# The second token group's sixteen gate tiles as three fp32r products of high and low parts

## The chip, the cores and the metric

The kernel runs on one core of a Trainium2 chip. The metric is the device time of one execution in microseconds (us). Five engines work side by side, each on its own queue of instructions in order: TensorE (PE, whose weight loads appear as PEld), VectorE (DVE), ScalarE (ACT), GpSimd (POOL) and SyncE (SP), which here only issues DMA transfers.

## The reference, cut to what matters

One layer of a hybrid decoder, for 512 prompt tokens and 64 sample tokens, model width 1024, float32 throughout:

```python
proj = x @ w_in
q, k, v, u, ga, gb = jnp.split(proj, SPLIT_IDX, axis=-1)      # ga, gb: 1024 columns each
a = attn_prompt(q, k, v, attn_sinks)                          # or attn_sample
s, hr, hi = ssm_branch(u, ...)
mix = jax.nn.sigmoid(ga) * (a @ w_attn_proj) + jax.nn.sigmoid(gb) * (s @ w_ssm_proj)
x = layer_norm(DN_ALPHA * x + mix @ w_out, ln1_g, ln1_b)
x = layer_norm(DN_ALPHA * x + peer(x, ...), ln2_g, ln2_b)
x = x + jax.nn.sigmoid(x @ ple_w_gate) * (p @ ple_w_proj)
```

The change concerns `sigmoid(ga)` and `sigmoid(gb)`. `peer` takes for each token the best 16 keys of two sets of 128 for each of 8 heads, the best 16 of their pair sums, and 128 experts that these name: a row of `u_tab` and one of `v_tab` for each.

## The kernel before, in words

The 576 tokens are two groups. Group A has 192 tokens (64 sample tokens and the first prompt block), group B has 384 (three prompt blocks of 128). Both go through the same steps, A first; B's steps are laid beside A's where the program allows it. Activations lie transposed, as 128 rows by 8 chunks by tokens.

**Gates.** `gate` (lines 526 to 531) makes `sigmoid(ga)` in eight tiles of 128 gate columns and `gate1` (lines 533 to 538) `sigmoid(gb)` in eight more, which only group B does this way. Each tile loads 128 x 1024 float32 weights (512 KB, `wload`, line 431, from a pool of six buffers), multiplies them with `g.xT` in eight chunks of 128 (`mm`, line 402, plain float32) into one PSUM tile of lane B, and ACT writes the sigmoid. The profile lists each plain float32 matmul as two records: the 128 matmuls of the sixteen tiles are 256 records. `g.xT` is B's input, 128 x 8 x 384 float32.

**Products of parts.** Elsewhere B's products are made of parts: ACT copies a float32 tile to the shorter format fp32r (the high part, line 213), DVE subtracts it from the tile (the low part, line 216), and three products are summed in PSUM: high with high, high with low, low with high (`mm3`, line 409; `parts` makes the two halves of a weight tile in lane H, whose pool `ws["H"]` has four buffers, two weight tiles with both halves). So the attention and SSM projections (`mix0`, `mix1`), the output projection (`out`, line 637), the PEER queries (`peerq`, 15 of its 16 tiles) and the experts (`up`, `dense`, lines 1127 and 1254) are made. `mix0` first makes parts of the attention output (`at`, line 543 and following, tag "xl" of the pool `xp`).

**Rows.** For the first two token blocks (A's) the experts' rows are gathered one at a time: POOL issues an indirect DMA of 128 rows of 4 KB (512 KB, line 1064) into one of four buffers and DVE reduces it (line 1074, later 1083). These reductions are pinned to their order in the program. `pull(n)` writes n of them at a place in the program: two for each tile of `gate1` (PG = 2), one for each of the eight tiles of `mix0`, 1.5 for each of the eight of `mix1` and of the eight steps of `out`. That is 16 + 8 + 12 + 12 = 48 up to the end of `out`. The other 336 follow later, most of them beside the dense experts.

**Order.** The main program around the change is, in the order in which it is written: A's PEER queries (`peerq`, with `topk_sides`, lines 959 to 963, after each quarter: the best 16 of each set of keys, on DVE); A's `topk` for the second block (`run(A.topk(tk, (1,)))`), whose last result is the row indices `idx` (line 1018) on which the first gather waits; B's `gate` with steps of A's `topk` for the first block beside it; B's `gate1` with the rows; `load_y`, `glu`, `mix0`, `mix1`, `out`; then `ln1`, `project` (line 937), `peerq` and `topk` for B, the experts (`first`, `dense`) and the last layer norm. The framework fixes the order of each engine's instructions when the program is built, and may put later work ahead of earlier work that isn't ready. At run time each engine takes its queue strictly in that order.

**Memory.** B's tiles of 128 x 4 x 384 have the tag "mB" with four buffers: `qT`, `AT`, `yT`, `sT`. The pool `xp` (xB) is opened once A's pools are closed, in memory that A's tiles held; it has two buffers of 128 x 8 x 384, "xh" (first `g1`, the result of `gate1`) and "xl" (first `at`). The pool `wH1`, lane H's buffers for `mix0`, `mix1` and `out`, is opened after `glu`.

Of the kernel before, what the change touches and what calls it, by code (L numbers as in the profile page):

```python
# [7 lines left out]
FP = mybir.dt.float32  # L8
# [5 lines left out]
FR = mybir.dt.float32r  # L14
AF = mybir.ActivationFunctionType
# [184 lines left out]
def build(tc, I, O, dbg=None):  # L200
    nc = tc.nc
    V, S, G, T, SY = nc.vector, nc.scalar, nc.gpsimd, nc.tensor, nc.sync
    mult, add, sub = ALU.mult, ALU.add, ALU.subtract
# [5 lines left out]
    def act(out, in_, fn, **k):  # L209
        S.activation(out, in_, fn, **k)  # L210

    def copy(out, in_):
        S.activation(out, in_, AF.Copy)  # L213

    def tt(out, a, b, op, e=None):
        return (e or V).tensor_tensor(out, a, b, op=op)  # L216

    with (
# [172 lines left out]
        def phase1(pools):  # L391
            (c1, wk, gp, ws) = pools
            if 1:
# [24 lines left out]
                class Lane:  # L418

                    def __init__(l, name, cols):  # L420
                        l.name, l.cols = name, cols
# [27 lines left out]
                class Group:  # L449
                    def __init__(g, d, pool, ga):  # L450
                        g.__dict__.update(d)
                        g.first = g.name == "A"
                        g.pool = pool
                        g.ln = LA if g.first else LB
                        g.xT = g.big("xT")
                        SY.dma_start(g.xT, I["xT" + g.name])
                        g.cs = ga.tile([128, 2, g.N], FP, name="cs" + g.name)
                        g.qT = g.med("qT")
                        g.kT = gp.tile([128, g.N], FP, name="kT" + g.name)
                        g.Vn = {}  # L460

# [61 lines left out]
                                    S.dma_start(O["kp"], t)  # L523


                    def gate(g):

                        g.mx = g.big("mix")
                        for n in range(8):
                            act(g.mx[:, n], g.mm(g.ln.wload(I["w_in"][10 + n]), g.xT, 8), AF.Sigmoid)  # L530
                            yield

                    def gate1(g, xp):

                        g.g1 = xp.tile([128, 8, g.N], FP, name="g1", tag="xh")
                        for n in range(8):
                            act(g.g1[:, n], g.mm(g.ln.wload(I["w_in"][18 + n]), g.xT, 8), AF.Sigmoid)
                            yield

                    def half(g, w, n, x):  # L540
# [816 lines left out]
        left, right = ExitStack(), ExitStack()  # L1357

        def open_(st, name, bufs=1, side="left", **k):
            return st.enter_context(tc.tile_pool(name=name, bufs=bufs, side=side, **k))  # L1360
# [4 lines left out]
        ws = {"B": wb}  # L1365
        setup = ssm_setup()
        next(setup)
        Group, LA, LB, consts, project, (ssm_U, ssm_X, ssm_states, ssm_Y) = phase1((c1, wk, gp, ws))
        A = Group(GA, ga, ga)
        w = [LB.wload(I["w_in"][6])]  # L1370
        B = Group(GB, gp, ga)
# [30 lines left out]
        def beside(work, n):  # L1402
            for _ in work:
                due[1] += n
                while due[1] >= 1:
                    due[1] -= 1
                    next(sb, 0)
# [55 lines left out]
        xp = open_(xB, "xB", 1, "right")  # L1463
        rows.extend(gathered_rows(bi, gt, wk2) for bi in (1, 0))
        run(A.topk(tk, (1,)))
        sb = A.topk(tk, (0,))
        due[1] = 0
        beside(B.gate(), T0)
        for _ in B.gate1(xp):
            pull(PG)  # L1470
        B.load_y()
        beside(B.glu(), T1)
        wH1 = ExitStack()
        ws["H"] = open_(wH1, "wH1", 4, "right")
        for _ in B.mix0(xp):
            due[1] += T2
            while due[1] >= 1:
# [60 lines left out]
```

## Time and profile before

| | |
|---|---|
| median of 3 runs | 1915.37 us (1914.25 to 1915.6) |
| profiled execution | 1914.61 us, its span 1912.8 us |
| mean granted clock of TensorE | 0.972 of full speed |
| PE busy | 94% of the span |
| DVE busy | 77% |
| ACT busy | 40% |
| POOL busy | 31% |
| B's gates up to the end of `out` | from about 383 to 553 us |
| experts that only PE bounds | from about 945 to 1645 us |

The profile is of one execution. Busy time is the time in which an engine had an instruction under way. An idle time is put down to what ended it last. The granted clock is 1.00 at 2.4 GHz and 0.50 at 1.2 GHz. The shares over the whole span say little here, because the stages have different limits; the windows by stage say more.

### The profile page before, as it was taken

The page shows a single profiled execution, that of the slowest core. Times are in us where ns is not written, and L with a number is a line of the kernel's source. Part 1 is how long each engine was busy: PE and PEld are TensorE (multiplying, and loading weights), DVE is VectorE, ACT ScalarE, POOL GpSimd, SP SyncE. Part 2 cuts the span into 40 slices and gives each one's busy share as a digit, 9 for nine tenths or more (in the row PEclk, how much of TensorE's full clock was granted, in tenths as well). Part 3 has the DMA queues.
Part 4 walks back from the last instruction along what each step waited for, and adds up shares of the span by engine and source line. Part 5 has one row for each costly group of instructions (what it writes and reads, how often), then busy time and mean ns, then how long its engine had stood idle before and what let it go on. Part 6 is the DMA issues. An engine that isn't in the chain of part 4 may idle for free.

```text
span 1912.8 us, 26365 instructions
## 1 busy us (share of the span) xinstructions
PE 1805.5 (94%) x9506; PEld 1551.1 (81%) x9506; DVE 1480.8 (77%) x2965; ACT 768.6 (40%) x1144; POOL 585.7 (31%) x437
## 2 busy tenths in 40 slices
PE   6789999999898989999999999999999999999998
PEld 5668897855768847888899999999999999877886
DVE  8261235697997898998678888888888888798885
ACT  2112443142232237797833333333333333344332
POOL 4110000007341210000035554444446566343220
PEclk9888999999899989999999999999999999999999
DMA  6743446338886366676899999999999999999952
GB/s 205 239 149 91 169 149 216 105 127 306 311 308 246 124 205 212 235 253 229 300 348 358 353 348 342 339 341 344 339 348 335 347 338 332 327 396 360 378 187 75
DMA packets 207795, 512.29 MB, mean 268 GB/s; under 512 B 33328, under 2 KB 99904, under 8 KB 205600
## 3 DMA queue, kind: packets, MB, share of 16 engines
q1 hardware_dynamic: 142608, 303.28, 44.6%
q0 software_dynamic: 56160, 204.78, 29.7%
q10 hardware_dynamic: 8896, 2.56, 0.5%
q8 instruction: 74, 1.21, 0.2%
q14 instruction: 57, 0.47, 0.1%
HBM read 461.34 MB, written 50.71 MB: 268 GB/s over the span
## 4 chain that ended last, share of the span: by engine, by line
PE 66%; DVE 15%; DMA 8%; ACT 5%; issue 4%; POOL 1%; SPq 0%; ACTq 0%; DVEq 0%; POOLq 0%
PE psA L1254 12%; PE psB L1254 12%; PE psB L1127 11%; PE psA L1127 11%; PE psA L402 6%; DMA g<-u_tab,idx 3%; PE psB L402 2%; ACT Gs L210 2%; DVE eq L216 2%; PE psA L637 2%; DMA fr<-w_gate 2%; PE psA L409 1%; DVE s L216 1%; DMA ur<-u_t 1%; PE psA L937 1%
## 5 line engine op out<-in xcount | busy, mean ns | idle before, releaser
L1064 POOL DMA_INDIRECT g<-u_tab,idx x192 | 285.4, 1486 | 748.3 <-DVE scr L1074 454.8
L1064 POOL DMA_INDIRECT g<-v_tab,idx x192 | 256.6, 1336 | 343.5 <-DVE acc L1083 303.1
L1074 DVE SCALAR_TENSOR_TENSOR scr<-g,x 128x1024 bf16<-128x1024 f32 x192 | 234.1, 1219 | 28.5 <-DMA g<-u_tab,idx 26.8
L1083 DVE SCALAR_TENSOR_TENSOR acc<-g,hh,acc 128x1024 f32<-128x1024 f32 x190 | 244.7, 1288 | 6.5 <-DMA g<-v_tab,idx 4.8
L213 ACT ACTIVATE vh<-vr 128x1024 fp32r<-128x1024 f32 x128 | 135.8, 1061 | 161.3 <-PE psB L1254 141.5
L216 DVE TENSOR_TENSOR ul<-ur,uh 128x1024 fp32r<-128x1024 f32 x120 | 146.6, 1223 | 67.2 <-ACT uh L213 64.6
L213 ACT ACTIVATE uh<-ur 128x1024 fp32r<-128x1024 f32 x120 | 127.0, 1062 | 155.7 <-PE psA L1127 72.8
L216 DVE TENSOR_TENSOR vl<-vr,vh 128x1024 fp32r<-128x1024 f32 x128 | 156.0, 1219 | 10.7 <-ACT vh L213 10.7
L1254 PE MATMUL psA<-vh,wh 128*128 128x512 f32 x384 | 151.1, 393 | 5.8 <-ACT wh L213 5.8
L1254 PE MATMUL psA<-vl,wh 128*128 128x512 f32 x384 | 150.1, 391 | 0.0
L1254 PE MATMUL psB<-vl,wh 128*128 128x512 f32 x384 | 150.1, 391 | 0.0
L1254 PE MATMUL psB<-vh,wh 128*128 128x512 f32 x384 | 150.0, 391 | 0.0
L1254 PE MATMUL psB<-vh,wl 128*128 128x512 f32 x384 | 150.0, 391 | 0.0
L1254 PE MATMUL psA<-vh,wl 128*128 128x512 f32 x384 | 149.4, 389 | 0.0
L213 ACT ACTIVATE wh<-wt 128x384 fp32r<-128x384 f32 x128 | 67.0, 524 | 181.1 <-DVE wt L216 144.9
L402 PE MATMUL psB<-xTB,w 128*128 128x384 f32 x400 | 132.9, 487 | 0.0
L216 DVE TENSOR_TENSOR wl<-wt,wh 128x384 fp32r<-128x384 f32 x128 | 71.2, 556 | 57.8 <-ACT wh L213 48.7
L402 PEld LDWEIGHTS psB<-xTB,w 128*128 128x128 f32 x400 | 75.0, 190 | 48.9 <-issue 0.6
L1127 PE MATMUL psB<-xh,uh 128*128 128x384 f32 x480 | 96.9, 344 | 5.0 <-ACT Gs L210 4.5
L1127 PE MATMUL psA<-xh,uh 128*128 128x384 f32 x480 | 95.2, 339 | 3.9 <-ACT uh L213 3.9
L210 ACT ACTIVATE Gs<-psB 128x512 f32<-128x512 f32 x96 | 94.9, 1150 | 7.9 <-PE psB L1174 7.9
L1127 PE MATMUL psA<-xl,uh 128*128 128x384 f32 x480 | 95.3, 337 | 0.0
(370 smaller groups left out, 3775.8 us busy)
## 6 DMA issues: line engine op xcount, KB each, us to landing
ur<-u_t SPq DMA_DIRECT2D x128, 512.0 KB
vr<-v_tab SPq DMA_DIRECT2D x128, 512.0 KB
Gg<-Gs SPq DMA_DIRECT2D x12, 2048.0 KB
G<-Gg SPq DMA_DIRECT2D x32, 768.0 KB
w<-w_in SPq DMA_DIRECT2D x42, 512.0 KB
w<-w_q SPq DMA_DIRECT2D x32, 512.0 KB
w<-w_out SPq DMA_DIRECT2D x16, 512.0 KB
Hd<-gl SPq DMA_DIRECT2D x42, 192.0 KB
```

Of the source, the lines that this page charges most:

```text
L210: S.activation(out, in_, fn, **k)
L213: S.activation(out, in_, AF.Copy)
L216: return (e or V).tensor_tensor(out, a, b, op=op)
L402: T.matmul(out, w[:, k, :], x[:, k, :], start=(k == 0), stop=(k == kc - 1))
L409: T.matmul(out, a[:, k], b[:, k], start=f and k == 0, stop=l and k == kc - 1)
L637: T.matmul(p[bi][:n], a[:, k + i, c0:c0 + n], b[:, i], start=f and i == 0, stop=e and i == 1)
L937: T.matmul(p, t[bi // 4][:, bi % 4, k], w[hf][:, k], start=(k == 0), stop=(k == 1))
L1064: G.indirect_dma_start(out=t, out_offset=None, in_=I[tab], in_offset=bass.IndirectOffsetOnAxis(ap=IDX[bi][:, i:i + 1], axis=0))
L1074: pin(V.scalar_tensor_tensor(scr, t, 1.0, X1[bi], op0=mult, op1=mult, accum_out=hh[:, i:i + 1]))
L1083: pin(V.scalar_tensor_tensor(acc, t, hh[:, i:i + 1], acc, op0=mult, op1=add))
L1127: T.matmul(p, w[:, c * 128:c * 128 + 128], z[:, c], start=f and c == 0, stop=l and c == 7)
L1254: T.matmul(y[b][hf], x[:, bs], z[:, hf * 512:hf * 512 + 512], start=f, stop=l)
```

## The change

B's gate tiles become sums of three fp32r products. `xparts` splits B's input once: the high part goes into two tiles with the tag "mB" (taken when the group is made, ahead of `AT`, `yT` and `sT`), the low part into the buffer "xl" of `xp`. Each gate tile's weights are split by `parts` into lane H's buffers, so the pool `wH1` is opened ahead of the gates. Group A's gates stay as they were.

```diff
@@ Group.__init__
                         g.qT = g.med("qT")
+                        if not g.first:
+                            g.xTh = [g.pool.tile([128, 4, g.N], FR, tag="m" + g.name, name="xTh", bufs=4) for _ in range(2)]
                         g.kT = gp.tile([128, g.N], FP, name="kT" + g.name)
@@ methods of Group
+                    def xparts(g, xp):
+
+                        lo = xp.tile([128, 8, g.N], FR, name="xTl", tag="xl")
+                        for k in range(0, 8, 2):
+                            hi, sl = g.xTh[k // 4][:, k % 4:k % 4 + 2], slice(k, k + 2)
+                            copy(hi, g.xT[:, sl])
+                            tt(lo[:, sl], g.xT[:, sl], hi.bitcast(FP), sub)
+                        g.xp = [g.xTh[k // 4][:, k % 4] for k in range(8)], [lo[:, k] for k in range(8)]
+
+                    def gates(g, w):
+
+                        raw = g.ln.wload(w)
+                        if g.first:
+                            return g.mm(raw, g.xT, 8)
+                        p = g.ln.ps(g.N)
+                        (wh, wl), (xh, xl) = parts(raw), g.xp
+                        for a, b, f, l in ((wh, xh, True, False), (wh, xl, False, False), (wl, xh, False, True)):
+                            for k in range(8):
+                                T.matmul(p, a[:, k], b[k], start=f and k == 0, stop=l and k == 7)
+                        return p
+
                     def gate(g):
 
                         g.mx = g.big("mix")
                         for n in range(8):
-                            act(g.mx[:, n], g.mm(g.ln.wload(I["w_in"][10 + n]), g.xT, 8), AF.Sigmoid)
+                            act(g.mx[:, n], g.gates(I["w_in"][10 + n]), AF.Sigmoid)
                             yield
 
                     def gate1(g, xp):
 
                         g.g1 = xp.tile([128, 8, g.N], FP, name="g1", tag="xh")
                         for n in range(8):
-                            act(g.g1[:, n], g.mm(g.ln.wload(I["w_in"][18 + n]), g.xT, 8), AF.Sigmoid)
+                            act(g.g1[:, n], g.gates(I["w_in"][18 + n]), AF.Sigmoid)
                             yield
@@ main program
         due[1] = 0
+        wH1 = ExitStack()
+        ws["H"] = open_(wH1, "wH1", 4, "right")
+        B.xparts(xp)
         beside(B.gate(), T0)
         for _ in B.gate1(xp):
             pull(PG)
         B.load_y()
         beside(B.glu(), T1)
-        wH1 = ExitStack()
-        ws["H"] = open_(wH1, "wH1", 4, "right")
         for _ in B.mix0(xp):
```

## Rows read from the trace of the kernel before

**Rows 1.** The page's busy time by engine: busy us (share of span) xinstructions.

```profile
PE 1805.5 (94%) x9506; PEld 1551.1 (81%) x9506; DVE 1480.8 (77%) x2965; ACT 768.6 (40%) x1144; POOL 585.7 (31%) x437
```

**Rows 2.** Windows by stage: busy us (instructions) of each engine, granted clock, DMA share.

```profile
core 0: us, PE busy (x) PEld busy (x) DVE busy (x) ACT busy (x) POOL busy (x), PEclk, DMA share, GB/s
...
316.00:383.00 67.00, 67.00 (x374) 55.47 (x373) 37.56 (x215) 14.82 (x34) 0.00 (x0) 1.00 0.35 115
383.00:421.00 38.00, 38.00 (x120) 22.50 (x121) 37.04 (x200) 14.45 (x17) 0.00 (x0) 1.00 0.28 92
421.00:455.00 34.00, 34.00 (x107) 20.06 (x106) 29.48 (x87) 13.74 (x17) 21.38 (x15) 1.00 0.84 296
455.00:466.00 11.00, 11.00 (x38) 6.79 (x37) 7.55 (x13) 2.79 (x5) 7.88 (x5) 1.00 0.82 282
466.00:510.00 44.00, 34.52 (x181) 33.80 (x179) 40.16 (x72) 10.98 (x13) 21.33 (x19) 0.91 0.87 316
510.00:553.00 43.00, 38.61 (x153) 30.94 (x153) 39.19 (x61) 9.00 (x10) 22.23 (x19) 0.89 0.92 319
```

**Rows 3.** Waits of DVE, 383 to 553 us: us in total, times, longest.

```profile
DVE scr L1074 <- DMA g<-u_tab,idx: 11.5, 7, 3.5
DVE VE L959 <- ACT sc L213: 4.5, 1, 4.5
DVE st L216 <- ACT st L213: 3.3, 1, 3.3
```

**Rows 4.** Timeline of PE: start, us, instruction xrecords; gate matmuls of B.

```profile
316.38 6.62 PE L402 MATMUL psB<-xTB,w 128*128 128x384 f32 x20
...
323.56 0.91 PE L402 MATMUL psB<-xTB,w 128*128 128x384 f32 x2
...
383.18 71.76 PE L402 MATMUL psB<-xTB,w 128*128 128x384 f32 x222
```

**Rows 5.** Chain that ended last: start, us; 24 fp32r matmuls of an expert tile.

```profile
972.64 4.17 PE psA L1127 x24
```

**Rows 6.** Groups of DVE, 383 to 553 us: busy, mean ns | idle before.

```profile
L1074 DVE SCALAR_TENSOR_TENSOR scr<-g,x 128x1024 bf16<-128x1024 f32 x48 | 58.4, 1217 | 11.9 <-DMA g<-u_tab,idx 11.5
L216 DVE TENSOR_TENSOR wl<-w,wh 128x1024 fp32r<-128x1024 f32 x16 | 19.4, 1218 | 0.0
...
L216 DVE TENSOR_TENSOR at<-ATB,at 128x1536 fp32r<-128x1536 f32 x1 | 1.8, 1759 | 0.3 <-ACT mixB L210 0.3
```

**Rows 7.** Timeline of ACT: a copy to high parts of each size.

```profile
383.94 1.47 ACT L213 ACTIVATE at<-ATB 128x1536 fp32r<-128x1536 f32 x1
...
445.61 1.06 ACT L213 ACTIVATE wh<-w 128x1024 fp32r<-128x1024 f32 x1 [0.32 <-DMA w<-w_ap]
```

**Rows 8.** Timeline of DVE: key maxima of B's first query quarter, then weight splits.

```profile
600.21 0.49 DVE L959 MAX8 VE<-sc 128x8 f32<-128x128 f32 x2 [0.42 <-ACT sc L213]
...
612.61 0.28 DVE L959 MAX8 VE<-sc 128x8 f32<-128x128 f32 x1
613.78 1.22 DVE L216 TENSOR_TENSOR wl<-w,wh 128x1024 fp32r<-128x1024 f32 x1
```

**Rows 9.** Timeline of PE: the matmuls that waited for that split.

```profile
615.05 2.93 PE L409 MATMUL psA<-xh,wl 128*128 128x384 f32 x8 [2.66 <-DVE wl L216]
```

**Rows 10.** Timeline of DVE, 404 to 421 us: A's second topk, its last result.

```profile
404.64 1.00 DVE L216 TENSOR_TENSOR eq<-eq,CI 128x1664 uint16<-128x1664 uint16 x1
...
419.95 0.21 DVE L1018 CAST idx<-ef 128x128 int32<-128x128 f32 x1
```

**Rows 11.** Timeline of PE: the first matmuls after the wait in `mix0`.

```profile
479.14 2.93 PE L409 MATMUL psB<-at,wh 128*128 128x384 f32 x8 [5.55 <-ACT wh L213]
```

**Rows 12.** Timeline of POOL: GLU's copies behind gathers; a gather issue beside a weight split.

```profile
474.78 1.84 POOL L616 COPY sTB<-ev 128x384 f32<-128x384 f32 x4
483.87 1.70 POOL L1064 DMA_INDIRECT g<-u_tab,idx  x1 [7.25 <-DVE scr L1074]
486.61 0.94 POOL L1064 DMA_INDIRECT g<-u_tab,idx  x1 [1.04 <-DVE scr L1074]
```

**Rows 13.** Timeline of SP's queue: weight loads of the gates and of GLU.

```profile
371.80 52.54 SPq L431 DMA_DIRECT2D w<-w_in  x9
429.17 5.49 SPq L431 DMA_DIRECT2D w<-w_glu  x2
```

## The prediction, made before the changed kernel ran

> **What bounds the kernel now.** The page's first part comes first: PE is busy for 94% of the span and DVE for 77% [rows 1]. Taken alone, that says that any PE time saved is time saved. The windows by stage correct it [rows 2]. While the gates run, from 383 to 455 us, PE has no gap, but from 383 to 421 us DVE is busy for 37.04 of 38 us as well: it is at group A's top-k. From 466 to 553 us both have gaps, 13.9 us on PE and 7.65 us on DVE. Over the 170 us from 383 to 553 us, PE is busy for 38.00 + 34.00 + 11.00 + 34.52 + 38.61 = 156.1 us and DVE for 37.04 + 29.48 + 7.55 + 40.16 + 39.19 = 153.4 us. The two are level, and what the change takes from the one it gives to the other. DVE's 16.6 us of idle time in this stretch are mostly 11.5 us of waiting for gathered rows and one wait of 3.3 us for the GLU result [rows 3]. The wait of 4.5 us in the same list lies nearly all before 383 us. What follows 553 us on the path (B's layer norm, queries, top-k, experts) needs B's output projection, so a shift of that point goes through to the end.
>
> **What it removes.** 128 plain matmuls. A block of 222 records, or 111 matmuls, takes 71.76 us [rows 4], so one takes 0.646 us and all take 82.7 us. In their place come 384 fp32r matmuls of the same 128 x 384 shape. Twenty-four of these take 4.17 us in the expert stage at full clock [rows 5], or 0.174 us each: 66.7 us in all. PE's work falls by 16.0 us. The Trainium skill (FP8 and Floating Point Precision, section TensorE Precision Notes) counts plain float32 as four passes through the array, so that three single passes would save a quarter, 20.7 us as an estimate. The rows decide for 16.0: each pass of its own costs some 12 ns more than a quarter of a plain matmul.
>
> **What it moves on PE.** Of the gate matmuls 34 records, 17 matmuls, run before 383 us: one block of 20 records at 316 us, while A's layer norm is under way and PE has nothing else, and seven pairs slipped between A's queries [rows 4]. After the change a gate tile can't start there: its low parts lie in memory that A's pools hold until A's queries are done, near 383 us. So 17 x 0.646 = 11.0 us of PE work lose their place. The seven pairs, 4.5 us, no longer delay A's queries, which end near 378.5 us. PE alone would have 66.7 us of gates from there, and would end them at about 446 us (1 us to start) in place of 455 us.
>
> **What it adds on DVE.** Sixteen weight splits of 1.218 us [rows 6]. Neighbouring instructions overlap by some 0.07 us, so 1.15 us each and 18.4 us in all. Four splits of the input, 128 x 768: by the 1.759 us for 128 x 1536 [rows 6], 0.88 us each and 3.5 us in all. Together 21.9 us. The split of the attention output (1.76 us, now before 421 us) moves behind the last gate tile, because it shares the buffer "xl" with the input's low part; it stays within the stretch. Its 1.47 us copy on ACT and these 1.76 us are then due right after the gates, where GLU's matmuls, the 11 us from 455 to 466 us in [rows 2], cover them.
>
> **What it adds on ACT.** Sixteen copies of 1.06 us and four of 1.47 / 2 = 0.74 us [rows 7], 19.9 us. ACT is busy for 14.45 + 13.74 of 72 us there [rows 2]. I cost this at nothing: the cover is ACT's 44 us of idle time. If a copy stood in the queue ahead of a top-k step, it would add about 1 us to that step.
>
> **Queues.** SP's nine loads of gate weights from 371.8 us wait for raw buffers, and GLU's loads stand behind them [rows 13]. A raw buffer is now free after its split, not after its matmuls, so these loads wait for DVE, but no bytes are added. I cost it at nothing; its other bound is the time by which the splits are late, which is counted with DVE already. POOL gets no new instruction.
>
> **The sum.** DVE does its queue in order, and in the query stage of B the trace shows whose turn it is. The key maxima hold DVE from 600.21 to 613.78 us without one weight split among them, and PE waits 2.66 us for that split [rows 8, 9]. In 383 to 421 us the maxima and A's second top-k are just such earlier work, up to the row indices at 419.95 us [rows 10]. So gate splits get the gaps of that chain, and the rest comes after 421 us beside rows. DVE becomes the bound. Its work starts 4.5 us sooner (378.5 us) and amounts to 153.4 + 21.9 = 175.3 us plus the waits that stay. None of 16 us of waits would put the end at 553.8 us, 0.8 us later than now; all of them at 569.8 us, 16.8 us later. A row that is late is now often waited for while a split runs, so I keep the 3.3 us for GLU and about half of the 11.5 us, 9.6 us together: 563.4 us, **10.4 us later**. Half is a choice between those two ends. The profiled execution of 1914.61 us would become 1925.0 us, and as the median of the runs shown lies 0.76 us above it, the forecast is **1925.8 us**.
>
> **Rivals.**
>
> First, **PE starves at the start of the gates** (a worse case of the forecast). The input's low part is needed whole by every tile's second product. If its four splits get no place before the gaps of A's second top-k, from 404 us on [rows 10], PE can do only the high products of two tiles, 16 x 0.174 = 2.8 us, and idles for some 20 us. Sixteen tiles less that from about 406 us end at 470 us, 15 us later than now. After a wait of 5.55 us eight matmuls took 2.93 us, 0.366 us each, twice the time of full clock [rows 11]; such a return costs some 3 us. It would give 14 to 20 us, 1929 to 1935 us. For it: the closed block in [rows 8]. Against: later work does get into gaps (the attention split, [rows 6], ran among A's top-k), and part of the 15 us comes back in `mix0`, which has 5.55 us of waiting to lose.
>
> Second, **PE stays at half clock** through gates that are fed in pieces. The trace shows 0.91 and 0.89 as the mean granted clock of stages with such waits, not 0.50 [rows 2], so short waits cost single stretches. At the doubled time sixteen tiles would cost 66.7 us more, less what DVE makes PE wait anyway: some 1970 us. The Trainium skill (TensorE: Matmul & The Clock Gate, section HAM oscillation) tells of a kernel that throttled anew at every tile because it waited between tiles; this stage's windows don't show that.
>
> Third, **the splits find room and PE's gain counts** (the other side). If DVE's gaps take the four input splits by 381 us and one weight split every 4.17 us, gates end near 446 us, 9 us sooner, and with DVE slower afterwards 4 to 9 us remain: 1906 to 1911 us. It decides at one point: before 421 us nine tiles would need 3.5 + 9 x 1.15 = 13.9 us, where DVE has 1 us free [rows 2] plus the 1.76 us that move away and 4.5 us by which it starts sooner. Against it is the 6.6 us that are missing. For it: steps of A's first top-k in those 38 us can move back, into DVE's 4.5 us of gaps up to 455 us.
>
> Fourth, **it cancels out**: all waits for rows vanish under splits (0.8 us, above), within 3.8 us of now.
>
> A fifth, smaller one changes the size alone. A gather issue beside a weight split took 1.70 us, and 0.94 us apart from one [rows 12]; GLU's copies on POOL stand behind such gathers. Half of the splits fall among rows, 8 x 0.76 = 6.1 us on POOL, which has 12.6 us free from 421 to 455 us [rows 2]. I count nothing and keep 6 us for the range.
>
> **How the numbers follow.** About 0.2%, 3.8 us, is what a measurement of this kernel can tell from no change. The forecast gets 0.46, the starved start 0.25, half clock throughout 0.04, the cancelling case 0.13, PE's gain 0.12. Thus faster 0.12, same 0.13, slower 0.75. The range from 1912 to 1936 us holds the forecast with its two ends (1916.2 to 1932.2), the starved start and the cancelling case; PE's gain and half clock, 0.16, are left out.
>
> **What would show it.** Right: splits of gate weights on DVE, few before A's row indices, most after; PE waiting for `wl` or for the input's low part within the gates; A's queries ending some 4 us sooner; the last gate tile after 455 us, the end of `out` after 553 us by as much as the whole. Wrong: PE busy without gaps through the gates, or DVE with as much idle time up to 553 us as before. If the end of `out` shifts and the end of the execution doesn't, the step that fails is that the shift goes through.

## The result and the profile after

| | before | after |
|---|---|---|
| median, the two kernels in turn on one chip | 1914.81 us (1910.7 to 1915.6, 4 runs) | 1938.9 us (1935.3 to 1942.79, 4 runs) |
| ratio | | 1.0137, interval 1.0118 to 1.0156 |
| profiled execution | 1914.61 us | 1937.53 us, span 1935.8 us, granted clock 0.967 |
| end of B's gates (first GLU matmul) | 454.8 us | 489.5 us |
| end of `out` (first matmul of `project`) | 552.7 us | 577.8 us |

The change makes the kernel 1.4% slower. The end of `out` moved by 25.1 us and the end of the profiled execution by 22.9 us: nearly all of the loss arises before 578 us and goes through to the end, as the prediction had it, but the loss is over twice the 10.4 us forecast.

The page's busy times of the changed kernel [rows 1]:

```profile
PE 1797.7 (93%) x9634; PEld 1573.1 (81%) x9634; DVE 1501.6 (78%) x2985; ACT 788.0 (41%) x1164; POOL 603.7 (31%) x437
```

PE works 7.8 us less and DVE 20.8 us more. The first is half of what the change removes, and the windows of the changed kernel say why [rows 2]; the last of them reaches past 553 us because `out` does:

```profile
316.00:383.00 67.00, 58.74 (x340) 51.65 (x339) 38.30 (x216) 12.43 (x29) 0.00 (x0) 0.95 0.32 103
383.00:421.00 38.00, 19.64 (x71) 16.31 (x69) 36.30 (x178) 15.75 (x16) 0.00 (x0) 0.77 0.20 70
421.00:455.00 34.00, 27.56 (x149) 27.56 (x150) 33.57 (x108) 19.36 (x21) 7.59 (x5) 0.86 0.47 170
...
466.00:510.00 44.00, 39.89 (x200) 34.99 (x199) 34.55 (x49) 14.86 (x18) 24.96 (x18) 1.00 0.83 298
510.00:553.00 43.00, 36.16 (x181) 33.22 (x180) 42.97 (x72) 12.59 (x16) 18.09 (x16) 0.92 0.85 290
553.00:575.00 22.00, 20.47 (x89) 16.26 (x88) 19.63 (x31) 4.25 (x4) 14.21 (x11) 1.00 0.94 333
```

Read the first two columns after the length (PE) against the third (DVE). From 383 to 421 us PE is busy for 19.64 us where it was for 38.00, and at a granted clock of 0.77; DVE is as full as before. From 421 to 455 us DVE has lost its gaps (33.57 of 34 us; before 29.48). So PE now waits for DVE, and the waits of PE from 383 to 578 us name the operand:

```profile
PE psB L546 <- DVE wl L216: 20.7, 5, 10.9
PE psB L546 <- DVE xTl L216: 5.9, 1, 5.9
```

PE's timeline shows where in the gates (line 546 is the gates' matmul, line 717 A's queries, 660 `out`, 960 `project`):

```profile
323.81 3.16 PE L679 MATMUL psA<-c_ident,x 64*128 64x64 f32 x16 [6.32 <-DVE x L1077]
326.81 3.63 PE L402 MATMUL psA<-x1TA,w 128*128 128x192 f32 x16
...
335.58 2.77 PE L402 MATMUL psA<-x1TA,w 128*128 128x192 f32 x16
...
383.81 0.85 PE L717 MATMUL psA<-w,ev 128*64 128x128 f32 x4 [0.48 <-ACT ev L213]
...
395.79 3.14 PE L546 MATMUL psB<-xTl,wh 128*128 128x384 f32 x6 [5.91 <-DVE xTl L216]
...
410.76 2.93 PE L546 MATMUL psB<-xTh,wl 128*128 128x384 f32 x8 [4.79 <-DVE wl L216]
...
427.44 2.93 PE L546 MATMUL psB<-xTh,wl 128*128 128x384 f32 x8 [10.87 <-DVE wl L216]
...
485.28 1.55 PE L546 MATMUL psB<-xTh,wh 128*128 128x384 f32 x8
...
489.46 10.48 PE L402 MATMUL psB<-yTB,w 128*128 128x384 f32 x32
...
577.78 2.74 PE L960 MATMUL psA<-w,pt 128*128 128x512 f32 x6
```

The eight matmuls after the waits of 4.79 and 10.87 us took 2.93 us, near half clock, against 1.55 us for the eight at 485.28 us. The gates begin only once A's queries have ended. The last matmuls of A's queries start at 383.81 us; before they started at 382.50 us, so the queries did not end sooner:

```profile
382.50 0.85 PE L694 MATMUL psA<-w,ev 128*64 128x128 f32 x4
```

And DVE, its waits from 383 to 578 us [rows 3] and its timeline at the first split of the input, the second split of a weight tile and the last row index of A:

```profile
DVE scr L1097 <- DMA g<-u_tab,idx: 15.5, 13, 4.4
DVE xTl L216 <- PE psA L717: 4.1, 1, 4.1
DVE st L216 <- ACT st L213: 1.9, 1, 1.9
```

```profile
384.70 0.96 DVE L216 TENSOR_TENSOR xTl<-xTB,xTh 128x768 fp32r<-128x768 f32 x1 [4.08 <-PE psA L717]
...
409.49 1.22 DVE L216 TENSOR_TENSOR wl<-w,wh 128x1024 fp32r<-128x1024 f32 x1
...
424.02 0.20 DVE L1041 CAST idx<-ef 128x128 int32<-128x128 f32 x1
```

The indices come 4 us later than before [rows 10]. After the first four gathers, the fifth waits for the first row reduction to free a buffer, which seven splits and A's first top-k hold up until 451 us. POOL's timeline at the fifth gather, before and after:

```profile
430.46 2.62 POOL L1064 DMA_INDIRECT g<-u_tab,idx  x1 [4.48 <-DVE scr L1074]
```

```profile
451.94 4.91 POOL L1087 DMA_INDIRECT g<-u_tab,idx  x1 [21.23 <-DVE scr L1097]
```

### The profile page after: what moved, and what is told of

It is laid out like the page before. It is cut to its first block, busy times and chain, and to the rows that moved or that the text cites. A ratio compares the mean times of both kernels' runs of the same rounds, so it can differ in the third digit from the quotient of the medians.

```text
span 1935.8 us, 26676 instructions
## 1 busy us (share of the span) xinstructions
PE 1797.7 (93%) x9634; PEld 1573.1 (81%) x9634; DVE 1501.6 (78%) x2985; ACT 788.0 (41%) x1164; POOL 603.7 (31%) x437
## 4 chain that ended last, share of the span: by engine, by line
PE 64%; DVE 15%; DMA 7%; issue 6%; ACT 5%; POOL 2%; SPq 0%; POOLq 0%; ACTq 0%; DVEq 0%
PE psB L1277 11%; PE psA L1277 11%; PE psB L1150 11%; PE psA L1150 10%; PE psA L402 6%; ACT Gs L210 2%; DMA g<-u_tab,idx 2%; DVE eq L216 2%; PE psA L660 2%; PE psB L402 2%; DMA fr<-w_gate 1%; PE psA L409 1%; POOL g L1087 1%; DMA ur<-u_t 1%; DVE s L216 1%
## 5 line engine op out<-in xcount | busy, mean ns | idle before, releaser
L1087 POOL DMA_INDIRECT g<-v_tab,idx x192 | 267.5, 1393 | 331.2 <-DVE acc L1106 300.8
L213 ACT ACTIVATE wh<-w 128x1024 fp32r<-128x1024 f32 x55 | 57.9, 1057 | 100.0 <-DVE wl L216 20.0
L1150 PEld LDWEIGHTS psB<-xh,uh 128*128 128x128 f32 x480 | 86.1, 192 | 10.3 <-ACT Gs L210 5.7
```

The costliest lines, as they stand in the source:

```text
L1087: G.indirect_dma_start(out=t, out_offset=None, in_=I[tab], in_offset=bass.IndirectOffsetOnAxis(ap=IDX[bi][:, i:i + 1], axis=0))
L1150: T.matmul(p, w[:, c * 128:c * 128 + 128], z[:, c], start=f and c == 0, stop=l and c == 7)
```

## Experiments

The question was which of three things costs the 25 us: the work that DVE got (the theory of the forecast), PE starving at the start of the gates (the first rival, which the timeline seems to show outright), or where the splits stand in DVE's queue. All runs are read at the same place, from 383 us to the end of `out`, where DVE's busy and idle time add up to the stretch:

| kernel | ratio to before [95%] | median us | gates end | `out` ends | DVE busy | DVE idle |
|---|---|---|---|---|---|---|
| before | | 1914.81 | 454.8 | 552.7 | 153.1 | 16.6 |
| after | 1.0137 [1.0118, 1.0156] | 1938.9 | 489.5 | 577.8 | 175.0 | 19.8 |
| no_weight_low | 1.0017 [1.0002, 1.0032] | 1917.07 | 456.0 | 559.1 | 157.4 | 18.6 |
| input_split_only | 1.0011 [0.9997, 1.0025] | 1916.35 | 455.8 | 558.3 | 156.4 | 18.9 |
| gate1_only | 1.0093 [1.0059, 1.0128] | 1931.56 | 464.0 | 567.8 | 166.5 | 18.4 |
| gate_only | 1.0165 [1.0138, 1.0191] | 1945.17 | 494.2 | 584.4 | 166.4 | 35.0 |
| last_four | 1.0048 [1.0006, 1.009] | 1924.84 | 462.9 | 564.8 | 159.5 | 22.4 |
| gates_ahead | 1.0133 [1.0105, 1.0161] | 1938.29 | 470.2 | 578.9 | 175.9 | 20.1 |
| plain_gates_ahead | 1.0001 [0.9986, 1.0015] | 1913.46 | 455.4 | 552.7 | 153.3 | 16.4 |
| plain_idle_splits | 1.0102 [1.0074, 1.013] | 1935.35 | 480.1 | 575.0 | 174.8 | 17.2 |
| plain_16_idle_subs | 1.0132 [1.0077, 1.0187] | 1936.71 | 456.3 | 576.8 | 175.5 | 18.3 |
| plain_8_idle_subs | 1.0074 [1.0054, 1.0094] | 1928.75 | 456.3 | 566.9 | 166.1 | 17.8 |
| low_on_pool | 1.0146 [1.0116, 1.0176] | 1941.2 | 489.5 | 579.5 | 179.9 | 16.6 |
| rows_later | 1.0183 [1.0163, 1.0204] | 1947.78 | 482.1 | 569.9 | 155.0 | 31.9 |
| plain_rows_later | 1.0026 [1.0004, 1.0047] | 1918.32 | 457.2 | 547.3 | 135.7 | 28.7 |
| gates_ahead_rows_later | 1.0097 [1.007, 1.0124] | 1929.77 | 463.6 | 551.8 | 156.4 | 12.4 |
| plain_mix0 | 1.0033 [1.0018, 1.0048] | 1919.51 | 454.9 | 558.5 | 149.3 | 26.2 |
| plain_mix01 | 0.9998 [0.9982, 1.0013] | 1912.79 | 455.1 | 552.9 | 143.8 | 26.1 |

The four right-hand columns are in us and from each kernel's one profiled execution; the median and the ratio are from all its runs against runs of the kernel before on the same chip, so the medians of different rows can be from different chips.

### The subtractions of the weights alone (no_weight_low)

```diff
-                        (wh, wl), (xh, xl) = parts(raw), g.xp
-                        for a, b, f, l in ((wh, xh, True, False), (wh, xl, False, False), (wl, xh, False, True)):
+                        wh, spare = LH.wt("wh", dt=FR), LH.wt("wl", dt=FR)
+                        copy(wh, raw)
+                        xh, xl = g.xp
+                        for a, b, f, l in ((wh, xh, True, False), (wh, xl, False, False), (wh, xh, False, True)):
```

> The changed kernel without the sixteen weight subtractions on VectorE: the third product of each gate tile multiplies the high part of the weights with the high part of the input once more, so TensorE has the same 384 matmuls and ScalarE the same copies. Theory D (the weight subtractions stand behind A's top-k in VectorE's queue, and TensorE starves for them: 20.7 us of its waits in the gates): the waits for wl go, only those for the input's low part stay (some 6 us); gates end near 465 us instead of 489, end of the output projection 553 to 560, time 1912 to 1922 us. Rival P (the 17 early matmuls that lost their place and the half clock after the start are the loss, whatever VectorE does): gates still end after 475 us, time 1927 us or more.

The third product takes the high parts a second time, so the result lacks the low part of the weights. PE does as many matmuls of the same shape (384), the input split and all copies on ACT stay, only DVE's sixteen subtractions are gone. The kernel is 0.02 to 0.32% slower than before, and its median 22 us under that of the changed kernel. The whole stretch in one window, of the kernel before, of the changed one and of this one:

```profile
383.00:552.70 169.70, 155.83 (x593) 113.90 (x594) 153.11 (x427) 50.97 (x60) 72.53 (x55) 0.95 0.74 261
```

```profile
383.00:577.78 194.78, 157.50 (x759) 141.58 (x758) 175.01 (x445) 70.81 (x80) 73.08 (x55) 0.91 0.66 231
```

```profile
383.00:559.07 176.07, 156.83 (x756) 142.55 (x757) 157.43 (x431) 68.44 (x80) 74.73 (x56) 0.92 0.74 258
```

PE's, ACT's and POOL's columns are the same within 2.4 us in the second and third; DVE's differ by 17.6 us, and the length by 18.7 us. So neither ACT's 20 us of copies, nor the 17 early gate matmuls that lost their place, nor the shorter matmuls make most of the loss. But this run takes the starving away together with the work, and can't tell the two apart.

### Starving or work: the subtractions without a reader, and the gates ahead of the top-k

In input_split_only all gate tiles are plain again and the input is still split. Two runs add to it subtractions on DVE whose result nobody reads, one for each of the sixteen gate tiles or for the second eight. The edit against input_split_only, for the first eight tiles of the run with sixteen (the condition keeps it to group B):

```diff
+                            if not g.first and 0 + n >= 0:
+                                tt(LH.wt("wl", dt=FR), g.xT[:, :, 0:128], g.xT[:, :, 128:256], sub)
                             act(g.mx[:, n], g.mm(g.ln.wload(I["w_in"][10 + n]), g.xT, 8), AF.Sigmoid)
```

> All sixteen gate tiles plain as before; the input is still split (nothing reads the parts), the lane H buffers are opened ahead of the gates and the attention output's parts share the buffer with the input's low part. Theories D and P: the moves by themselves cost little, 0 to 5 us (1914 to 1920 us). Rival M (the moves of buffers make the loss): over 1925 us.

> The run with plain gates and the input's split (1916 us, output projection's end at 558 us), with one subtraction of 128 x 1024 more on VectorE for each of the sixteen gate tiles. It reads two slices of the input and nothing reads its result, so no other engine waits for it. Theory L: 18.4 us of work on the engine that sets the end of this stretch: the output projection ends 572 to 580 us, 1930 to 1938 us, as in the changed kernel. Rival S (starving of TensorE): TensorE's gates run on until 456 us as before, 1916 to 1921 us.

> The same with eight, in the second eight gate tiles alone. Theory L: half of it, 9.2 us: 564 to 571 us, 1922 to 1929 us, in line with the kernel whose second eight tiles are made of parts (568 us, 1931.6 us). Rival S: 1916 to 1919 us.

The run with sixteen (plain_16_idle_subs) settles the question. PE starts its gates as before, runs 222 records without a gap and ends them at 456.3 us, 33 us before the changed kernel does. `out` still ends at 576.8 us, 1.0 us before that of the changed kernel, and the time is 1936.71 us. With eight, `out` ends 14.2 us later than before and the time is 1928.75 us. The window of the stretch, PE's gates, its longest wait and the group of the idle subtractions, of the kernel with sixteen:

```profile
383.00:576.77 193.77, 161.29 (x599) 115.95 (x599) 175.49 (x447) 50.01 (x60) 78.21 (x56) 0.93 0.67 229
```

```profile
384.74 71.76 PE L402 MATMUL psB<-xTB,w 128*128 128x384 f32 x222
```

```profile
PE psB L409 <- DVE at L216: 13.7, 1, 13.7
```

```profile
L216 DVE TENSOR_TENSOR wl<-xTB 128x1024 fp32r<-128x1024 f32 x16 | 19.3, 1209 | 0.0
```

PE, well ahead after its gates, gives its lead back at the next thing that DVE makes, the split of the attention output: one wait of 13.7 us. DVE's work of 175.5 us and 18.3 us of its waits are the length.

The converse keeps the whole change and lets PE starve less: the gates are written ahead of A's second top-k.

```diff
-        run(A.topk(tk, (1,)))
-        sb = A.topk(tk, (0,))
...
-        beside(B.gate(), T0)
+        t1 = A.topk(tk, (1,))
+        for _ in B.gate():
+            next(t1, 0)
+        run(t1)
+        sb = A.topk(tk, (0,))
         for _ in B.gate1(xp):
+            due[1] += T0
+            while due[1] >= 1:
+                due[1] -= 1
+                next(sb, 0)
             pull(PG)
```

> The changed kernel with the same instructions, but A's second top-k is written beside the first eight gate tiles (one step after each tile) instead of ahead of them, and A's first top-k beside the second eight. VectorE has the same work in another order. Theory D-order (the weight splits stand behind the top-k in VectorE's queue; the place costs, not the amount): TensorE's waits for wl in the gates fall from 20.7 us to under 6, gates end 12 to 20 us sooner than in the changed kernel; the row indices come some 8 us later than 425 us; 1912 to 1925 us. Rival D-load (VectorE is simply full from 383 us to the output projection, in whatever order): within 4 us of the changed kernel, 1935 to 1943 us.

> The kernel before, plain gates, with the same other place of the two top-ks: the control for the run above. As plain gate tiles ask nothing of VectorE, both theories expect little: the row indices wait for some gate steps in the program but for none in VectorE's queue; 1912 to 1919 us.

The waits of PE for splits within the gates fall from 26.6 to 10.6 us, and the gates end 19 us sooner than in the changed kernel. The end of `out` is the same within 1.2 us, and so is the time. The same order with plain gates costs nothing. One thing besides the waits differs: A's row indices come at 431.1 us in gates_ahead, 7.1 us later than in the changed kernel, and at 420.6 us in the control, so the control doesn't price that delay. The first row reduction comes sooner all the same (438.1 us, and 450.5 us in the changed kernel). Waits of PE and the window of gates_ahead:

```profile
PE psB L660 <- ACT wh L213: 6.4, 1, 6.4
PE psB L409 <- ACT wh L213: 6.2, 2, 6.0
PE psB L546 <- DVE xTl L216: 5.8, 1, 5.8
PE psB L546 <- DVE wl L216: 4.8, 2, 4.5
```

```profile
383.00:578.93 195.93, 160.68 (x758) 142.97 (x757) 175.87 (x448) 69.30 (x80) 76.29 (x56) 0.90 0.70 236
```

The starving is real, but here it is idle time of an engine that isn't the bound. What PE saves at the gates it loses later, behind parts that aren't ready.

### Half of the change, and a quarter

Plain gates for the first eight tiles (gate1_only), for the second eight (gate_only), or for all but the last four (last_four, the diff; `i` is the number of the tile):

```diff
-                        if g.first:
+                        if g.first or i < 12:
                             return g.mm(raw, g.xT, 8)
```

> Products of parts only in the second eight gate tiles; the first eight are plain float32 as before, the input is split. Theory D: the first tiles need nothing from VectorE and keep TensorE busy while A's top-k runs, the eight later splits fall among the rows; early matmuls are back; 1908 to 1920 us, near the kernel before. Rival V (VectorE's added work counts wherever it stands, 8 x 1.15 + 3.5 = 12.7 us): 1922 to 1930 us.

> Products of parts only in the first eight gate tiles; the second eight are plain. Theory D: most of the loss is here, 15 to 25 us over the kernel before (1929 to 1940 us), less what plain tiles of the second eight can fill while the first ones wait. Rival V: 12.7 us, near 1927 us, as with the other eight.

> Products of parts only in the last four of the sixteen gate tiles; the other twelve are plain and keep TensorE busy until some 434 us, when A's second top-k is over (row indices at 420 to 425 us). Theory D-order: no tile waits for a top-k, four tiles save 4 us on TensorE and cost 8.1 us on VectorE; 1912 to 1919 us. Theory D-load: half of the loss of the second eight (17 us) and more, 1922 to 1925 us.

With gate1_only, eight splits cost as much as the eight idle subtractions, within 1 us at the end of `out`. It isn't the other half that gate_only gives: DVE's work is the same (166.4 and 166.5 us), but `out` ends at 584.4 us, 6.6 us later than with all sixteen and 16.6 us later than with gate1_only. PE's timeline there, the end of the split tiles and the plain ones after them:

```profile
444.53 1.55 PE L546 MATMUL psB<-xTh,wh 128*128 128x384 f32 x8
...
448.71 1.55 PE L546 MATMUL psB<-xTh,wh 128*128 128x384 f32 x8
...
452.89 41.44 PE L402 MATMUL psB<-xTB,w 128*128 128x384 f32 x128
```

The tiles that starve come first, and eight plain ones of 5.2 us each are left for PE after them; now DVE waits (35.0 us in the stretch). This agrees with starving that costs where DVE has room, but doesn't show it alone: the 17 early gate matmuls, 11.0 us of PE, run before 383 us in gate1_only and within the stretch in gate_only. Neither time fits an expectation: 1931.56 us lies above rival V's range, 1945.17 us above theory D's. In last_four the four weight splits and the input's four raise DVE's work by only 6.3 us, while `out` ends 12.1 us later: 5.8 us of it are waits that grew, those for rows to 19.0 us. So a split's cost isn't its 1.15 us alone; the waits for rows move with it by several us either way.

### The splits with plain products (plain_idle_splits), and on POOL (low_on_pool)

```diff
-                        (wh, wl), (xh, xl) = parts(raw), g.xp
-                        for a, b, f, l in ((wh, xh, True, False), (wh, xl, False, False), (wl, xh, False, True)):
-                            for k in range(8):
-                                T.matmul(p, a[:, k], b[k], start=f and k == 0, stop=l and k == 7)
+                        parts(raw)
+                        mm(p, raw, g.xT, 8)
```

```diff
-                        (wh, wl), (xh, xl) = parts(raw), g.xp
+                        wh, wl = LH.wt("wh", dt=FR), LH.wt("wl", dt=FR)
+                        copy(wh, raw)
+                        tt(wl, raw, wh.bitcast(FP), sub, G)
+                        xh, xl = g.xp
```

> All sixteen gate tiles are plain float32 products, but each tile's weights are split all the same (16 copies on ScalarE, 16 subtractions on VectorE, the input's split) and nothing reads the parts. TensorE never waits for a split; VectorE has the changed kernel's work. Theory L (VectorE is full from 383 us to the end of the output projection, so its added 18.4 us come out at that end, wherever they stand and whoever waits): end of the output projection 570 us or later, 1928 to 1938 us. Rival S (the loss is TensorE starving and cooling at the start of the gates): near the run with the input's split alone, 1916 to 1921 us.

> The changed kernel with the sixteen gate weight subtractions on GpSimd instead of VectorE; GpSimd is idle until the row indices are there. By the 128 x 384 additions of the trace (1.0 us) one takes some 2.7 us, less than the 4.17 us that TensorE takes for a tile. Both theories: VectorE is relieved, so the waits for wl before 425 us go and the gates end near 465 us; after that the row gathers stand behind subtractions in GpSimd's queue. If that costs little, 1912 to 1920 us as without the weight subtractions (1917); if the gathers are held up, 1922 to 1932 us.

The first gives most of the loss without the products, but isn't clean: the splits hold the raw buffers, and PE waits 17.2 us for weight loads that it doesn't wait for in the kernel before. The idle subtractions above, which read B's input in place of the weights, were made for that reason.

The second was to take 18 us off DVE. DVE's busy time rose instead, from 175.0 to 179.9 us, and nothing was won. Two groups of DVE from 383 to 580 us, before and in low_on_pool (busy us, mean ns):

```profile
L216 DVE TENSOR_TENSOR eq<-eq,CI 64x1664 uint16<-64x1664 uint16 x4 | 4.0, 1007 | 0.0
...
L216 DVE TENSOR_TENSOR eq<-eq 64x832 uint16<-64x832 uint16 x4 | 2.3, 578 | 0.0
```

```profile
L216 DVE TENSOR_TENSOR eq<-eq 64x832 uint16<-64x832 uint16 x4 | 6.7, 1680 | 0.0
L216 DVE TENSOR_TENSOR eq<-eq,CI 64x1664 uint16<-64x1664 uint16 x4 | 6.1, 1525 | 0.0
```

POOL's sixteen subtractions took 2.64 us on average. Beside them the same DVE instructions of A's top-k take up to three times as long on average; one of them, beside the POOL subtraction that it overlaps:

```profile
437.64 2.40 POOL L216 TENSOR_TENSOR wl<-w,wh 128x1024 fp32r<-128x1024 f32 x1
```

```profile
437.85 3.07 DVE L216 TENSOR_TENSOR eq<-eq,CI 64x1664 uint16<-64x1664 uint16 x1
```

The work was moved off DVE, but more than it came back as longer instructions. The time, 1941.2 us, is 9 us above the upper of the two ranges expected.

### Room on DVE: the rows moved to the experts

```diff
-P0, P1, P2, P3, P4, PG = 1, 1.5, 3, 3, 1.5, 2
+P0, P1, P2, P3, P4, PG = 1, 1.5, 3, 3, 1.5, 0
-PULL1, PULL3, PULL4, PULL5 = 0.25, 3, 1, 2
+PULL1, PULL3, PULL4, PULL5 = 0.25, 3.2, 1, 2
```

Sixteen row reductions leave the gates and are done beside the dense experts, in the changed kernel (rows_later), in the kernel before (plain_rows_later), and with the gates ahead as well.

> The changed kernel with the 16 rows of the second eight gate tiles moved into the expert stage (none per gate tile, 3.2 in place of 3 per expert step), where TensorE alone bounds and VectorE is idle for 115 of 700 us. Theory L: 16 x 1.22 = 19.5 us of VectorE leave the stretch, the end of the output projection comes 12 to 20 us sooner than 578 us, 1917 to 1928 us. Rival S: the waits at the start of the gates are before the first row, so they stay; at most the 15.5 us of waits for rows shrink by a third: 1932 to 1938 us.

> The kernel before with the same 16 rows moved: the control. Theory L: TensorE has no gap in its plain gates until 465 us, so only the 14 us of TensorE's gaps from 466 to 553 us can go; 1905 to 1914 us. If the expert stage can't take the rows for nothing, 1914 to 1920 us.

> Both: the top-ks written beside the gates and the 16 rows moved. Gates that ended at 470 us with the rows in place, and VectorE relieved of 19.5 us. Theory L: 1912 to 1925 us, no better than the run with the rows moved alone by more than 5 us, since the order doesn't change the amount. Rival S: the starved start is gone as well and TensorE's 16 us of saved work come out: 1900 to 1910 us.

The windows of rows_later and of gates_ahead_rows_later:

```profile
383.00:569.93 186.93, 156.86 (x752) 141.97 (x753) 154.99 (x412) 68.81 (x77) 42.88 (x39) 0.90 0.57 195
```

```profile
383.00:551.75 168.75, 153.59 (x756) 138.69 (x757) 156.38 (x415) 69.09 (x79) 44.46 (x40) 0.94 0.63 218
```

DVE's work is now 155.0 and 156.4 us, near that of the kernel before, and only now does the order of the gates matter: 18 us at the end of `out` and 18 us of time (1947.78 and 1929.77 us). Theory L, by which the order gains no more than 5 us, and rival S, by which the kernel comes to 1900 to 1910 us, both missed; rows_later itself came out above both of its ranges. So both readings of the trace hold, each in its place: with DVE full, its work decides and the starving is free; with room on DVE, the starving decides. With both cured, `out` ends at 551.8 us, 1 us sooner than before the change. The kernel is still 1% slower, because the experts don't take the rows for nothing. From the end of `out` to the end of the profiled span the three kernels with moved rows need 1370.8 to 1374.1 us; the other fifteen kernels of the table, whose rows stay, need 1355.4 to 1361.1 us (1360.1 before). That is also why rows_later is slower than the changed kernel, though its `out` ends 7.9 us sooner, and why plain_rows_later, whose `out` ends 5.4 us sooner than before, comes out slower by 0.04 to 0.47%.

### The other direction: less work on DVE than before

`mix0` made of plain products, without any splits, in the kernel before, and then `mix1` as well (the same edit there); the edit of `mix0`:

```diff
-                        if not g.first:
-                            x = xp.tile([128, 2, 4, g.N], FR, name="at", tag="xl")
-                            copy(x[:, 0], g.AT)
-                            tt(x[:, 1], g.AT, x[:, 0].bitcast(FP), sub)
-                            x = x[:, 0], x[:, 1]
...
-                                w = w if g.first else parts(w)
-                            tt(g.mx[:, n], g.half(w, n, x), g.mx[:, n], mult)
+                            tt(g.mx[:, n], g.mm(w[:, n % 2 * 4:], x, 4), g.mx[:, n], mult)
```

> The kernel before with the attention projection of the second group in plain float32: 4 weight splits (4.6 us) and the split of the attention output (1.76 us) leave VectorE, 6.4 us; TensorE gets 32 matmuls of 0.646 for 96 of 0.174 us, 4.0 us more. Theory L: the output projection ends 3 to 7 us sooner (546 to 550 us), 1908 to 1912 us. Rival T (below its present amount VectorE isn't the bound, TensorE is): 553 to 557 us, 1914 to 1919 us.

> Both projections in plain float32: 12.7 us off VectorE (some 140 us busy left), 8.0 us more on TensorE (some 164 us of 170). Theory L with TensorE as the next bound: 545 to 552 us, 1907 to 1914 us. Rival T: 557 to 562 us, 1918 to 1924 us.

If DVE's work alone set the end, these had to be faster. They aren't: one is 0.18 to 0.48% slower, the other the same. The ends of `out`, 558.5 and 552.9 us, lie outside every range expected for them. DVE's work fell by 3.8 and 9.3 us and its idle time rose by as much or more. Waits of DVE in plain_mix0, and the window of plain_mix01:

```profile
DVE scr L1068 <- DMA g<-u_tab,idx: 20.1, 15, 2.3
```

```profile
383.00:552.85 169.85, 160.50 (x530) 100.93 (x530) 143.79 (x420) 41.61 (x51) 63.70 (x56) 0.98 0.75 262
```

In the second PE is busy for 160.5 of 169.85 us. Up from the kernel before, with the rows in place, `out` moved by 1.0 to 1.9 us for each us of DVE's work that was added (2.4 in gate_only). Down from it little or nothing comes back: 17.4 us less in plain_rows_later gave 5.4 us, and 9.3 us less here gave none; both runs of this section also give PE more to do, so they don't tell PE's part from that of the rows. Why the waits for rows rise in plain_mix0 stays open. No kernel of the study beats the one before.

## Why the prediction was wrong in size and right in kind

**DVE becomes the bound, and the shift goes through: shown.** Sixteen subtractions that nobody waits for make the same loss as the change, eight make over half of it (the input's splits are in both), and with the weights' subtractions gone little is left. DVE's work in the stretch was forecast at 175.3 us and measured at 175.0. Of the 25.1 us at the end of `out`, 22.9 us are left at the end of the execution. In all kernels whose rows stay in place, what follows `out` takes the same within 6 us (above); a small shift can be lost in that: 6.4 us in no_weight_low left a time 0.02 to 0.32% above before.

**The step that failed is the sum's last: where DVE starts and how much it waits.** 378.5 + 175.3 + 9.6 = 563.4 us was forecast, 383.0 + 175.0 + 19.8 = 577.8 us measured. The 14.4 us between them are 4.5 us of the start, 10.2 us of the waits, and 0.3 us the other way. Of the waits' 10.2 us, 9.2 us are rows: the 9.6 us kept were 3.3 us for GLU and 6.3 us for rows, and 15.5 us of rows came.

- *"Its work starts 4.5 us sooner"* was wrong. The seven pairs of gate matmuls between A's queries had stood in places where PE waits for ACT anyway: five waits of 0.42 to 0.48 us for `ev` appear there now. And without the block at 316 us, PE idled for 6.32 us, and A's first 16 query records then took 3.63 us where 16 further on take 2.77 us (granted clock 0.95 in this window, 1.00 before). Work that fills gaps isn't a delay, and taking it out gave nothing: the last of A's queries came 1.3 us later.
- *"About half of the 11.5 us"* of waits for rows was wrong; so was the reason, that a row would arrive while a split runs. 15.5 us were measured, in 13 waits in place of 7. The splits delay the reductions, a reduction frees the buffer for a later gather, and that gather then starts later too: at 451.94 us for the fifth, 430.46 us before. In ten of the eleven other kernels of the table that kept all the rows and had at least the DVE work of before, DVE's idle time was 16.4 to 22.4 us; more work never hid it. (The waits for rows within it are not as steady: 9.4 us in plain_idle_splits, 19.0 us in last_four.) The forecast's own upper end, which keeps 16 us of waits, was 569.8 us; with the start put right it is 574.3 us.

**PE's saving** was right: 4.18 us for a tile of 24 matmuls at full clock (485.28 to 489.46 us), 0.174 us each. That PE was nevertheless busy for 157.5 us in the stretch, where 156.1 − 16.0 + 11.0 = 151.1 follows, is the half clock after the waits: the 384 gate matmuls kept PE busy for 76.4 us in place of 66.7, at a granted clock of 0.87; the matmuls after them for 80.0 us, and 84.1 us before. The window of the gates alone, PE and PEld:

```profile
383.00:489.46 106.46, 76.37 (x384) 72.89 (x384) 0.87 0.48 169
```

**ACT** was busy for 19.8 us more, as worked out (19.9), and the run without weight subtractions keeps the copies and shows that they cost nearly nothing: its `out` ends 0.7 us after that of input_split_only, which has none of the weights' copies (its gate products are plain). **POOL's** busy time didn't change (72.5 and 73.1 us), so the 6 us of the fifth rival did not come.

**The rivals.** The starved start happened, for 26.6 us where 20 us were worked out, and its mechanism was still the wrong one for the time: the end of the gates moved by 34.7 us, that of `out` by 25.1. It was given 14 to 20 us; in these runs it decides only where DVE has room. Half clock throughout didn't come: 0.77 and 0.86 in the two worst windows, 1.00 or 0.92 later. PE's gain and the cancelling case fell with the waits.

Of the signs named, splits of the weights mostly after the row indices (14 of 16), waits of PE within the gates and the later ends of the gates and of `out` came; A's queries ending 4 us sooner did not. "DVE with as much idle time as before" was named as a sign of being wrong. It came (19.8 us, and 16.6 us before) and marks the step that failed, though it made the loss larger than forecast and not smaller.

## What to carry to other kernels

Where two engines are level over a stretch, the stretch takes the fuller one's work plus its waits; keep the waits in full unless a row shows what will hide them, above all where the late thing is itself released by the engine that gets the work. To tell the cause of a wait from its cost, add the suspected work without a reader: if the end moves as far with nobody waiting, the visible wait isn't what costs the time there. Work that sits in another lane's gaps is free there, and moving it away gains nothing in the lane that it left.

## What was not expected of the hardware

Elementwise work on POOL lengthened DVE's instructions: on average 578 to 1680 ns and 1007 to 1525 ns (low_on_pool, above), so that DVE was busy for 4.9 us more after losing sixteen subtractions. The Trainium skill (SBUF — State Buffer, section SBUF: two separate sides) describes a pair of ports that the two engines share and that one of them holds for a whole instruction while the other is blocked; a DVE operation with two inputs in SBUF is among those concerned, but only against a POOL operation that reads SBUF, as these subtractions do. The rows of low_on_pool agree with that: the DVE instruction at 437.85 us, which takes about 1.0 us before the change, ends at 440.92 us, 0.9 us after POOL's subtraction. Where the other instructions' time went was not followed one by one.

A gather's issue on POOL took up to 4.91 us in the changed kernel and up to 4.45 us before, where others took 0.94 us [rows 12]; whether DVE's instructions held it up was not tried.
